# Output projections of retention heads 0 and 1 as one product of quarters in seven parts

## The chip, the cores and the metric

The kernel runs on one core of one Trainium2 chip. The time is that of the whole program on the device in microseconds (us), and three runs of the kernel before gave a median of 869.23 us (868.9 to 870.93). One more execution was taken with the hardware profiler: it took 870.49 us, and its span, from the first to the last instruction, is 868.7 us. The core has five engines that run side by side, each in the order of its own instructions: PE (TensorE, the matrix products), DVE (VectorE), ACT (ScalarE), POOL (GpSimd, here only a queue for transfers) and SP (SyncE, the queue for nearly all loads).

## The reference

The reference is a backbone of two layers over 512 tokens of width 1024, with 256 context tokens in front, all in float32. Layer 0 is a retention mixer with four heads, layer 1 a gated mixer in chunks of 128 tokens. The change touches the end of layer 0:

```python
ox, _, _ = retention_bidirectional(qx, kx, vx, log_g, s_f, s_b)   # (1, 4 heads, 512 tokens, 512)
out_x = retention_output(ox, zx, w_out)

def retention_output(o, z, w_out):
    o = o * lax.rsqrt(jnp.mean(o * o, axis=-1, keepdims=True) + NORM_EPS)
    b, h, l, dv = o.shape
    o = o.transpose(0, 2, 1, 3).reshape(b, l, h * dv).astype(z.dtype)
    return (o * jax.nn.silu(z)) @ w_out            # w_out: (4 heads * 512, 1024)

x = x + gate_x[:, None] * out_x
```

The product with `w_out` is a sum over the heads: each head adds its normalised and gated output (512 tokens by 512) times its own 512 rows of `w_out`.

## The kernel before

**Numbers as pairs.** A float32 number is held as two values of the type float32r, a high and a low part, and a product of two such numbers takes three matrix instructions (`mm3`): low by high, high by low, high by high. Whatever goes into PE is therefore split first: ACT copies the high part (a CAST in the profile) and DVE subtracts it from the source to get the low part (`split`). Weights come from memory as tiles `raw` of 128 by 1024 numbers (512 KB) and are split into tiles `hl`, of which there are four (`HL = 4`), used in turn.

**Products in seven parts.** The large projections (query, key, value and gate of layer 0, the value and u/z projections of layer 1) are computed as products of two by two quarters with seven products in place of eight. Tokens and inner dimension of the activations are halved into A11, A12, A21, A22, the weights into B11, B12, B21, B22. The sums of quarters of the activations are S1 to S4, those of the weights T1 to T4. `Product.run` takes one of seven names at a time and multiplies: B11 by A11, B21 by A12, T1 by S1, T2 by S2, B22 by S4, T3 by S3, T4 by A22. Partial results are taken out of PSUM by ACT (`snap`) and joined to the later ones by DVE (`plus`); `done` is called with each finished quarter. In a pair (`PAIRED`), two such products go through the names side by side, so that each operand has twice the time to be made.

**The stream of weights.** `Stream` (`Q`) holds the order in which the quarters of the weights are consumed. `load` sends a raw tile as soon as one of its slots is free; `get` hands out the next split tile and has the splits of the two after it written; the sums T1, T2 and T4 are made by DVE in place (`Q.sum`), and T3 by a transfer that adds in place, issued by POOL (`Q.add`, line 186).

**The heads.** After all projections (their results lie in DRAM) comes a loop over the four heads, lines 1306 to 1311. `attend(h)` has six steps of scores (12 products of 128 by 256 on PE, then on DVE the factor of the decay, `pf`, then a split, `ph` and `pl`), and two steps behind each comes its product with the values (12 products of 128 by 512). Six steps are two halves of the tokens (`hf`) times three pairs of key tiles. When a half is done, `finish` squares it on ACT to get the norm, `gated` multiplies by norm and gate on DVE (`gt`), and `flip` turns it on PE with transposes and splits it into the operand `og`. `project_out(h)` multiplies `og` with the head's four tiles of `w_out`, half by half: 2 halves x 4 tiles x 2 columns of 128 x 12 = 192 products of 128 by 256. Each group of 12 is added by DVE to the tile `acc`, which was loaded with x: `acc = p * gate0 + acc` (line 1302).

**What runs beside it.** Loading and splitting of the next head's queries and keys (`load_qk`), values (`load_v`), its decay table (`decay`) and its output weights (`load_wo`) are generators. `aside` takes one step of one of them and pins its ACT and DVE instructions behind what was written last on that engine (`pinned`). `bg` makes the modulation vectors of both layers on DVE from a stream of rows (`ada_piece`); its last piece (gate of layer 1) runs beside the heads, a step at a time (`step`).

**What sets the order.** PE's instructions stay in the order of the text. On the other engines a planner (the compiler's tile scheduler) picks, whenever it thinks an engine free, the instruction that is ready and stands first in the text; only pinned instructions and those behind a fence keep to the order of the text among themselves. All waits come from the tiles: a tile that takes a slot waits for the last reader of the tile before it in that slot. The slot is named by the tag in `st(shape, tag)`.

Nearly all compute instructions carry line 54 in the profile (the helper that records them), so groups are told apart by tile names.

Of the kernel before, what the change touches and what calls it, by code (L numbers as in the profile page):

```python
# [67 lines left out]
def hybrid_kernel(ctx, tc, xT_d, cT_d, cv_d, sv_d, rows_d, ada0_d, adag_d, w_d, rope_d, dec_d, ws_d, id_d, out_d):  # L68
# [21 lines left out]
    def lay(sizes, bufs=1):  # L90
        for tag, n in sizes.items():
# [4 lines left out]
         "sh1": 32, "shs": 16, "la": 32, "lb": 32, "lc": 32, "sum0": 16, "sum1": 16, "bns": 768, "mv": 32, "rv": 16})  # L96
# [6 lines left out]
    lay({"s0": 4096, "s2": 4096, "s3": 4096, "rope": 4096, "w6": 4096, "g2": 4096, "hl0": 8320})  # L103

    lay({"t2": 2048}, T2)
    lay({"hl1": 8320, "hl2": 8320, "hl3": 8320})
# [48 lines left out]
    class Stream:  # L155
# [23 lines left out]
        def add(self, must=None):  # L179

            for e in list(self.due):
                q = e[0]
                if (q, "22") in self.raws and (q == must or self.tick > e[1]):
                    self.due.remove(e)
                    self.added.add(q)
                    nc.gpsimd.dma_start(self.raws[q, "12"], self.raws[q, "22"], accum_op=ALU.add)  # L186
# [19 lines left out]
        def upto(self, n, late=None):  # L206

            while self.done < min(n, self.limit or len(self.items)):
# [4 lines left out]
                if name == "T3":  # L213
                    if q not in self.added:
                        self.add(q)
                    assert q in self.added
# [20 lines left out]
        def sum(self, n):  # L237
# [4 lines left out]
            if name == "T3" or name[0] not in ("T", "gated") or any((q, u) not in self.raws for u in uses):  # L242
                return
# [9 lines left out]
            if name == "T1":  # L253
                self.due.append((q, self.tick))
# [27 lines left out]
    def parts_of(q, u):  # L282
# [9 lines left out]
        if kind == "v1":  # L292
            return wide_parts(64 + 4 * i, kh, nh)
        return narrow_parts(80 + 2 * i + nh, 96 + 2 * i + nh, kh)
# [24 lines left out]

    FIRST_V1 = len(Q.items)  # L320
    V1_SLOTS = W + ["dec", "rope", "g0", "g2", "g3"]
    for a, b in ((0, 1), (2, 3)):
# [4 lines left out]
        for u in ("11", "21", "12", "22"):  # L327
            for cb in (a, b):
                Q.load((("v1", cb), u), V1_SLOTS, 2, parts_of(("v1", cb), u))

    def add_out(p, js=range(4)):
        for j in js:
# [3 lines left out]
            Q.load((q, "w"), W, 2, [(lambda r, e=e: r[:, 512 * e:512 * e + 512], w_d[112 + 4 * p + 2 * (j % 2) + e][:, h:h + 512])  # L336
# [3 lines left out]
    for i in range(UZ):  # L340
        Q.quad(("u", i), SINGLE)
        for u in RAWS:
            Q.load((("u", i), u), W, 2, parts_of(("u", i), u))
# [695 lines left out]
    def decay(h, tags=("w1", "g0")):  # L1039
        dt = dts[h] = st([P, TW], "dec", name="dt")  # L1040
        es = []
        for i in range(3):
# [8 lines left out]
            if n:  # L1051
                dve.tensor_tensor(dt[:, o:o + n], e[:, 0:n], e[:, 512:512 + n], ALU.mult)
# [703 lines left out]
```

## Time and profile before

| what | value |
| --- | --- |
| median of three runs | 869.23 us (868.9 to 870.93) |
| profiled execution, its span | 870.49 us, 868.7 us |
| PE busy | 858.7 us, 99% of the span |
| DVE busy | 698.8 us, 80% |
| ACT busy | 461.4 us, 53% |
| POOL busy | 78.1 us, 9% |
| scores and values of head 0 | 328.25 to 354.16 us |
| output projection of head 0 | 354.16 to 377.07 us |
| scores and values of head 1 | 377.07 to 403.34 us |
| output projection of head 1 | 403.34 to 426.26 us |
| heads 2 and 3 | 426.26 to 527.62 us |

The granted TensorE clock is 0.998 of full speed over the span. In the rows of groups "x12" counts instructions, the number behind the bar is their busy time in us and then the mean of one in ns; behind the second bar stands how long the engine was idle just before them and what ended most of that. In a timeline a row is a run of like instructions: start, length, engine, tiles written <- tiles read, count, and in brackets the idle time before it. Matrix instructions overlap, so the pace of PE is read from the distance of starts and not from the mean of one. "hl_e", "oA", "oS" and "og" are operands of PE, "pst" is any PSUM bank, "bg" a row tile of the modulation or decay stream.

### The profile page before, as it was taken

To read this page: it belongs to the slowest core of one execution; us is meant where nothing else is said; L and a number is where in the kernel's file an instruction comes from. 1 tells how busy PE (TensorE), PEld (TensorE's weight loads), DVE (VectorE), ACT (ScalarE), POOL (GpSimd) and SP (SyncE) were. 2 spreads that over 40 slices of the span, in tenths; PEclk is the share of its full clock that TensorE was granted. 3 is DMA by queue.
4 is the path that set the end of the run, shared out by engine and by line. 5 is a ranking of instruction groups with operands and counts; after the bars stand their busy time and mean duration, and the time that the engine had idled before them with its cause. 6 is when DMAs were issued, how large, how long until landed. Compare 5 with 4: busy or idle time off the path is not lost.

```text
span 868.7 us, 17062 instructions
## 1 busy us (share of the span) xinstructions
PE 858.7 (99%) x6870; PEld 822.4 (95%) x6870; DVE 698.8 (80%) x1007; ACT 461.4 (53%) x724; POOL 78.1 (9%) x119
## 2 busy tenths in 40 slices
PE   8999999999999999999999999999999999999997
PEld 7899999999999999999989899999999899899986
DVE  4799899869968885878676669998888478678895
ACT  4566644464364445627363649744667456255434
POOL 0001211211211011000000002021000000000110
PEclk9999999999999999999999999999999999999999
DMA  9945857868967898757174623666556246156522
GB/s 356 405 128 149 255 179 258 263 205 234 308 187 227 248 320 297 249 168 248 55 232 133 216 51 110 218 161 216 171 146 192 51 147 204 39 146 194 121 43 104
DMA packets 77551, 165.88 MB, mean 191 GB/s; under 512 B 8096, under 2 KB 33184, under 8 KB 77472
## 3 DMA queue, kind: packets, MB, share of 16 engines
q1 hardware_dynamic: 65856, 128.40, 44.8%
q0 software_dynamic: 11184, 36.18, 16.0%
q8 instruction: 54, 0.88, 0.4%
q10 hardware_dynamic: 432, 0.20, 0.1%
q14 instruction: 25, 0.20, 0.1%
HBM read 128.58 MB, written 24.12 MB: 176 GB/s over the span
## 4 chain that ended last, share of the span: by engine, by line
PE 94%; DMA 2%; DVE 1%; ACT 1%; issue 1%; ACTq 0%; DVEq 0%
PE pst L54 94%; DMA bg<-in_dec_dram 1%; DMA ident<-in_id_dram 1%; ACT junk L54 0%; DMA bg<-in_adag_dram 0%; DVE o L54 0%; ACT bg L54 0%; DVE acc L54 0%; DVE v L54 0%; DVE ada_a L54 0%; ACT L54 0%; DVE hl L54 0%; ACT hl L54 0%; ACT fss L54 0%; DVE dt L54 0%
## 5 line engine op out<-in xcount | busy, mean ns | idle before, releaser
L54 DVE TENSOR_TENSOR hl<-raw,hl 128x1024 fp32r<-128x1024 f32 (+2 forms) x197 | 235.8, 1200 | 69.3 <-ACT hl L54 69.0
L54 ACT CAST hl<-raw 128x1024 fp32r<-128x1024 f32 (+2 forms) x197 | 202.1, 1030 | 142.2 <-PE pst L54 60.9
L54 PE MATMUL pst<-hl,oS 128*128 128x256 f32 x1152 | 135.0, 277 | 0.0
L54 PEld LDWEIGHTS pst<-hl,oS 128*128 128x128 f32 x1152 | 132.9, 188 | 0.8 <-ACT ctx L54 0.4
L54 PE MATMUL pst<-oS,hl 128*128 128x256 f32 x1104 | 132.2, 277 | 0.0
L54 PEld LDWEIGHTS pst<-oS,hl 128*128 128x128 f32 x1104 | 128.1, 188 | 0.8 <-issue 0.8
L54 PE MATMUL pst<-oA,hl 128*128 128x256 f32 x936 | 116.9, 280 | 0.1
L54 PEld LDWEIGHTS pst<-oA,hl 128*128 128x128 f32 x936 | 110.7, 188 | 2.0 <-ACT oS L54 0.4
L54 PE MATMUL pst<-hl,oA 128*128 128x256 f32 x768 | 92.4, 277 | 0.0
L54 PE MATMUL pst<-og,hl 128*128 128x256 f32 x768 | 91.1, 278 | 0.0
L54 PEld LDWEIGHTS pst<-og,hl 128*128 128x128 f32 x768 | 89.2, 188 | 0.3
L54 PEld LDWEIGHTS pst<-hl,oA 128*128 128x128 f32 x768 | 89.4, 188 | 0.0
L54 DVE TENSOR_TENSOR raw<-raw 128x1024 f32<-128x1024 f32 x69 | 84.2, 1221 | 0.8
L54 ACT ACTIVATE snap<-pst 128x512 f32<-128x512 f32 x75 | 44.7, 596 | 69.3 <-PE pst L54 69.3
L54 PE MATMUL pst<-v,ph 128*128 128x512 f32 x192 | 59.8, 392 | 0.0
L54 PE MATMUL pst<-hl,ya 128*128 128x512 f32 (+1 forms) x246 | 59.1, 386 | 0.0
L186 POOL DMA_DIRECT2D raw<-raw x23 | 20.1, 874 | 388.5 <-ACT hl_e L54 173.4
L54 PEld LDWEIGHTS pst<-hl,ya 128*128 128x128 f32 x246 | 45.3, 188 | 9.5
L54 DVE TENSOR_TENSOR snap<-snap,pst 128x512 f32<-128x512 f32 x69 | 47.1, 682 | 5.7 <-PE pst L54 5.5
L54 ACT CAST ph<-pf 128x512 fp32r<-128x512 f32 x24 | 14.8, 618 | 56.3 <-DVE pf L54 56.3
L54 PEld LDWEIGHTS pst<-v,ph 128*128 128x128 f32 x192 | 36.1, 188 | 7.1
L54 DVE SCALAR_TENSOR_TENSOR acc<-pst,gate,acc 128x256 f32<-128x256 f32 x64 | 29.3, 480 | 11.5 <-PE pst L54 11.4
(207 smaller groups left out, 1106.4 us busy)
## 6 DMA issues: line engine op xcount, KB each, us to landing
raw<-in_w_dram SPq DMA_DIRECT2D x224, 256.0 KB, 4.0
bg<-in_adag_dram SPq DMA_DIRECT2D x32, 512.0 KB, 5.1
raw<-raw POOLq DMA_DIRECT2D x23, 512.0 KB, 4.8
ada_w<-in_ada_dram SPq DMA_DIRECT2D x16, 512.0 KB, 8.5
raw<-in_w_dram SPq DMA_DIRECT2D x16, 512.0 KB, 4.7
bg<-in_dec_dram SPq DMA_DIRECT2D x12, 512.0 KB, 4.5
v<-snap POOLq DMA_DIRECT2D x16, 256.0 KB, 4.2
z<-snap POOLq DMA_DIRECT2D x16, 256.0 KB, 4.5
```

The costliest lines, as they stand in the source:

```text
L54: made = op(*args, **kw)
L186: nc.gpsimd.dma_start(self.raws[q, "12"], self.raws[q, "22"], accum_op=ALU.add)
```

## The change

The output projections of heads 0 and 1 are taken out of the loop over heads and become one product of an activation matrix of 512 tokens by 1024 (head 0's 512 and head 1's 512) with the 1024 by 1024 rows of `w_out` that belong to these heads. It is done in quarters (token half by head, head by half of the columns) with seven products, as a pair of two column groups (`OUT0`), 14 items of 24 matrix products. The scores and values of both heads now come first, in one run of 12 steps (`attend_two`), the output product behind both (`out_two`). Heads 2 and 3 stay as they were (`attend_one`, `project_out`).

What it moves and adds:

- `flip` no longer writes `og` but hands the turned half to a function of its quarter, which splits it (A11, A12, A22), keeps plain copies and makes the sums S1 to S4 on DVE and ACT, pinned in order.
- The weights of both heads go through the stream `Q`: 8 raw tiles as before, but 14 splits in place of 8, with sums T1 and T2 on DVE and T3 and T4 by adding transfers from POOL. Three raw tiles are loaded at step 7 and five at step 11, when the slots of head 1's queries and keys come free.
- The finished quarters are written to `acc` by ACT, scaled by `gate0` (`put`), in place of DVE's multiply-add; x is added to `acc` behind that by four transfers from POOL that add in place, in place of four plain loads from SP before.
- A plan (a dictionary of steps) says which generator steps run where. Head 1's values take slots of the `hl` tiles and its decay table the slots `s0` and `s2`. Head 2's queries and keys are loaded and partly split during the 12 steps, its values and decay table during the output product.
- `bg`'s last piece moves from heads 0 to 2 to heads 2 and 3.
- The stream's free slots are emptied behind the output product, so that the first loads of layer 1's weights later take the slots `dec`, `rope`, `g0`, `g2` and `g3` first.

The diff, cut to what matters:

```diff
+    OUT0 = (("wo", 0), ("wo", 1))
+    WO_RAWS = ["w0", "w1", "w2"]
+    for name in PAIRED:
+        for q in OUT0:
+            Q.item(q, name)
+    for u in ("11", "21", "12", "22"):
+        for q in OUT0:
+            Q.load((q, u), WO_RAWS + list(ODD), 2, parts_of(q, u))
...
+    def outward(bank, a, w, fresh):
+        for kt in range(4):
+            if kt == 2 and inside:
+                inside.pop(0)()
+            r = (a[:, 0, kt, :], a[:, 1, kt, :])
+            for s in range(2):
+                o = kt * HS + s * P
+                mm3(bank[:, s * HS:s * HS + HS], (w[:, 0, o:o + P], w[:, 1, o:o + P]), r, fresh and kt == 0 and s == 0, kt == 3)
...
+        ROOM = {"A11": "oS3", "S3": "oS4", "A12": "oA12", "A22": "oA22", "S1": "oA11", "S2": "oS1", "S4": "oS2"}
...
+        def turn(h, hf, flipped):
+            act.pinned = dve.pinned = True
+            (quarter_11, quarter_21, quarter_12, quarter_22)[2 * h + hf](flipped)
+            act.pinned = dve.pinned = False
+        def quarter_11(flipped):
+            halved_parts("A11", flipped)
+            for r, src in zip(plain("11", "w3"), flipped):
+                act.copy(r, src)
+        def quarter_21(flipped):
+            for r, src in zip(parts("11"), flipped):
+                dve.tensor_tensor(r, r, src, ALU.subtract)
+            for r, src in zip(plain("21", "dec"), flipped):
+                act.copy(r, src)
+            halved("S3", at["11"])
+        def quarter_12(flipped):
+            halved_parts("A12", flipped)
+            for r, x, src in zip(plain("12", "g1"), parts("11"), flipped):
+                dve.tensor_tensor(r, x, src, ALU.subtract)
+        def quarter_22(flipped):
+            for r, src in zip(parts("21"), flipped):
+                dve.tensor_tensor(r, src, r, ALU.subtract)
+            halved("S1", at["21"])
+            for r, src in zip(parts("11"), flipped):
+                dve.scalar_tensor_tensor(r, src, -1.0, r, ALU.mult, ALU.subtract)
+            halved("S2", at["11"])
+            for r, src in zip(parts("12"), flipped):
+                dve.tensor_tensor(r, src, r, ALU.add)
+            halved("S4", at["12"])
+            halved_parts("A22", flipped)
...
+        plan = {(0, 2): [q, q, q, d], (1, 2): [d, v], (2, 2): [d, q, v], (3, 2): [q, q, v], (4, 1): [q], (5, 2): [v],
+                (6, 2): [q, v, q2, q2, q2], (7, 1): [v, raws], (8, 1): [v], (10, 1): [q2, q2],
+                (11, 2): [more, ahead(1)], (12, 2): [q2, ahead(2)]}
+        return attend((0, 1), plan, turn)
+    def out_two(flip, works):
+        def put(c):
+            def done(name, t):
+                th, nh = int(name[0]) - 1, int(name[1]) - 1
+                for s in range(2):
+                    m = 2 * (c + 2 * nh) + s
+                    act.activation(acc[:, m, th * HS:th * HS + HS], t[:, s * HS:s * HS + HS], AF.Copy, scale=gate0[:, m:m + 1])
+            return done
+        def turned():
+            flip()
+            between_modes()
+        prods = {q: Product(outward, put(q[1])) for q in OUT0}
+        n = 0
+        for name in PAIRED:
+            for q in OUT0:
+                w = Q.get()
+                if n == 1:
+                    inside.append(turned)
+                prods[q].run(name, w)
+                for work in works.get(n, ()):
+                    aside(work)
+                n += 1
+        Q.free[:] = []
+        for c in range(4):
+            nc.gpsimd.dma_start(acc[:, 2 * c:2 * c + 2, :], xT_d[:, 2 * c:2 * c + 2, :], accum_op=ALU.add)
...
-                if then is None and hf == 1 and c < 3:
+                if then is None and hf == 1:
                     step()
...
+    qs, ds, vs = load_qk(2), decay(2, ("w3", "g1")), load_v(2)
+    flip = attend_two(load_qk(1), load_v(1), decay(1, ("w3", "g1")), qs)
+    out_two(flip, {6: (vs, ds), 8: (vs, qs), 9: (ds,), 10: (vs, qs), 11: (vs, ds), 12: (vs, qs), 13: (vs, vs)})
     Q.limit = None
-    for h in range(HEADS - 1):
-        qs, vs = load_qk(h + 1), load_v(h + 1)
-        og, flip = attend(h, qs, vs)
-        project_out(wos.pop(h), og, flip, (decay(h + 1), vs, qs))
-    og, flip = attend(HEADS - 1, iter(()), iter(()))
+    qs, vs = load_qk(3), load_v(3)
+    og, flip = attend_one(2, qs, vs, load_wo(2), (2, 3, 5, 6))
+    project_out(wos.pop(2), og, flip, (decay(3, ("s0", "s2")), vs, qs))
+    og, flip = attend_one(3, iter(()), iter(()), load_wo(3), (0, 1, 2, 3, 5, 6))
```

In `attend` of both versions the flip of a half comes two steps behind its last value product; in the run of 12 steps that is at steps 6, 9 and 12 (`if i % 3 == 0 and pend`), and the fourth half is turned inside the second item of the output product (`turned`, called by `outward` after half of its matrix products).

More of the change, by code (lines that the diff above doesn't have):

```diff
@@ L1037, in hybrid_kernel, with decay @@
     dts = {}
[L1039 to L1040 removed]
+    def decay(h, tags):
+        if h == 1:
+            xt, ct = st([P, XW], "s0", name="dt"), st([P, CW], "s2", name="dt")
+        else:
+            whole = st([P, TW], "dec", name="dt")
+            xt, ct = whole[:, 0:XW], whole[:, XW:]
+        dts[h] = xt, ct
         es = []
@@ L1262, in attend @@
                 continue
-            if i == len(steps):
+            if i % 3 == 0 and pend:
                 flip()
-            aside(qs)
-            if i > 4:
-                aside(vs)
-            if (h, i) == (0, 2):
-                sp.pinned = True
-                for c in range(4):
-                    load(acc[:, 2 * c:2 * c + 2, :], xT_d[:, 2 * c:2 * c + 2, :])
-                sp.pinned = False
-            if i < 5:
-                aside(wo)
-            if i in (3, 5, 6):
-                step()
@@ L1277, in attend, with attend_one @@
-        return og, flip
+            run((i, 2))
+        return flip
+    def attend_one(h, qs, vs, wo, steps):
+        og = [st([P, 2, 4, HS], tag, F32R, name="og") for tag in ("oS3", "oS4")]
+        def turn(h, hf, flipped):
+            for fp, src in enumerate(flipped):
+                split((og[hf][:, 0, 2 * fp:2 * fp + 2, :], og[hf][:, 1, 2 * fp:2 * fp + 2, :]), src)
+        of = lambda work: lambda: aside(work)
+        plan = {(5, 0): [of(qs), of(wo)]}
+        for i in range(8):
+            plan[i, 2] = [of(qs)] + ([of(vs)] if i > 4 else []) + ([of(wo)] if i < 5 else []) + ([step] if i in steps else [])
+        return og, attend((h,), plan, turn)
```

172 lines of the change are left out of this document (112 added, 60 removed).

## The prediction

> **What bounds the kernel now.** I read the page first, then PE's waits, then the timeline of PE over heads 0 and 1, then each engine's busy time by stage.
>
> ```profile
> span 868.7 us, 17062 instructions
> PE 858.7 (99%) x6870; PEld 822.4 (95%) x6870; DVE 698.8 (80%) x1007; ACT 461.4 (53%) x724; POOL 78.1 (9%) x119
> PE 94%; DMA 2%; DVE 1%; ACT 1%; issue 1%; ACTq 0%; DVEq 0%
> ...
> PE pst L54 <- DMA ident<-in_id_dram: 1.9, 1, 1.9
> ...
> PE pst L54 <- DVE pf L54: 0.2, 1, 0.2
> ```
>
> PE is busy for 858.7 of 868.7 us, and the chain that ended last is PE for 94%. The one wait of PE among the heads is that of 0.2 us for `pf`. So a matrix product that is left out shortens the span by its pace on PE, unless its operands come late.
>
> ```profile
> 354.16 5.61 PE L54 MATMUL pst<-og,hl 128*128 128x256 f32 x48
> 359.61 1.03 PE L54 MATMUL pst<-ident,gt 128*128 128x128 f32 x8
> 360.40 0.95 PE L54 MATMUL pst<-og,hl 128*128 128x256 f32 x6
> 361.19 0.38 PE L54 MATMUL pst<-ones 128*128 128x128 f32 x2
> 361.33 15.90 PE L54 MATMUL pst<-og,hl 128*128 128x256 f32 x138
> 377.07 2.88 PE L54 MATMUL pst<-qk 128*128 128x256 f32 x24
> 380.17 1.65 PE L54 MATMUL pst<-qk 128*128 128x256 f32 x12 [0.22 <-DVE pf L54]
> ```
>
> This is head 0's output projection. From start to start 48 products take 5.45 us and 138 take 15.74 us, 113.5 and 114.1 ns each; I use 113.8. A flip costs 0.79, the two products on `ones` behind it 0.14.
>
> **The change, part by part: PE.** Two projections of 192 products become 14 items of 24, 336 in all: 48 x 0.1138 = 5.46 us less. The four flips of the two heads remain, three now among the scores; one pair on `ones` goes, 0.14. Head 1's scores follow head 0's in one run, so the start of head 1 with its 0.22 goes. Together 5.8 us. The output product lasts 336 x 0.1138 + 0.79 + 0.14 = 39.2 us. Counted from its start, item n begins at 2.73 n, and 0.93 later from item 2 on.
>
> **VectorE during the output product.** First what its operations take:
>
> ```profile
> L54 DVE TENSOR_TENSOR hl<-raw,hl 128x1024 fp32r<-128x1024 f32 x191 | 232.8, 1222 | 67.3 <-ACT hl L54 67.1
> L54 DVE TENSOR_TENSOR raw<-raw 128x1024 f32<-128x1024 f32 x69 | 84.2, 1221 | 0.8
> L54 DVE TENSOR_TENSOR snap<-snap,pst 128x512 f32<-128x512 f32 x69 | 47.1, 682 | 5.7 <-PE pst L54 5.5
> L54 DVE SCALAR_TENSOR_TENSOR acc<-pst,gate,acc 128x256 f32<-128x256 f32 x64 | 29.3, 480 | 11.5 <-PE pst L54 11.4
> L54 DVE TENSOR_TENSOR og<-pst,og 128x512 fp32r<-128x512 f32 x16 | 10.3, 685 | 0.5 <-ACT og L54 0.5
> ...
> 354.16:377.07 22.91, 2.37 (x5) 1.00 0.60 212
> ...
> 355.61 1.41 DVE L54 SCALAR_TENSOR_TENSOR gt<-pst,ss,z 128x512 f32<-128x512 f32 x2
> ```
>
> The row with 2.37 (x5) is the decay table of one head. Two of the 14 splits lie ahead of the product. What is left for VectorE inside it, in us: 12 low halves 14.7; four sums T1 and T2 4.9; six joins at 0.682 4.1; six quarter sums behind the last flip 4.1; low halves of S1, S2, S4 3.7 and of A22 1.4; `gt` 1.4; of head 2 the values 3.7, two key tiles 1.4 (like hl's and og's shapes) and the decay table 2.4. Taken out: 32 additions to `acc`, 15.4. The sum is 41.8 us in 45 instructions. Instructions in a queue overlap in the records: two `gt` of 0.745 take 1.41, 0.08 less each, so the sum is 41.8 - 3.6 = 38.2 of 39.2 us. VectorE is nearly full there. Has this kernel had that without loss?
>
> ```profile
> core 0: us, PE busy (x) PEld busy (x) DVE busy (x) ACT busy (x) POOL busy (x), PEclk, DMA share, GB/s
> 354.16:377.07 22.91, 22.91 (x204) 22.91 (x202) 17.64 (x31) 10.67 (x18) 0.00 (x0) 1.00 0.60 212
> 403.34:426.26 22.92, 22.92 (x204) 22.92 (x203) 18.52 (x33) 11.81 (x20) 0.00 (x0) 1.00 0.44 156
> 426.26:475.68 49.42, 49.42 (x360) 46.20 (x359) 34.65 (x57) 24.73 (x40) 0.00 (x0) 1.00 0.50 160
> 540.00:560.00 20.00, 20.00 (x173) 19.99 (x172) 20.00 (x27) 17.01 (x25) 1.93 (x4) 1.00 0.58 187
> 560.00:580.00 20.00, 20.00 (x177) 20.00 (x177) 20.00 (x30) 9.62 (x12) 4.30 (x7) 1.00 0.80 226
> ```
>
> From 540 to 580 us VectorE is full for 40 of 40 us, making S1 to S4 beside a pair of products just as here, and PE has no idle time. So a full VectorE alone costs nothing; late operands would. The tightest point is item 8 (B22 by S4), at 22.8: until then VectorE owes 1.4 for `gt`, seven low halves 8.6, four sums 4.9, two joins 1.4, six quarter sums 4.1, three S halves 3.7, in all 24.1 less 24 x 0.08 = 22.2 of 22.8. This holds only if the three waits for ScalarE's high halves of S1, S2 and S4 are filled with weights' work. Bounds: 0 if they are, 3.1 (three times 1.05, the cast below) if none is. I take 0.5, near the filled case, because the trace just shown is nearest to it.
>
> The fourth flip comes 36 products after the last value product (item 0 and half of item 1, 4.1 us) where it came after 48 (5.45). `gt` ended at 357.02, 2.86 after 354.16. Of the slack 1.2 us remain, so it costs nothing; VectorE brings little backlog there: steps 8 to 11 of the scores last 4 x 4.2 and hold four `pf` and `pl`, two pairs of `gt`, one quarter's sums and some splits, by the rows above about 14 us. Without that cover each us late is a us on PE.
>
> **ScalarE during the output product.**
>
> ```profile
> L54 ACT CAST hl<-raw 128x1024 fp32r<-128x1024 f32 x191 | 199.4, 1048 | 142.2 <-PE pst L54 60.9 <-DVE raw L54 54.0 <-issue 18.6
> L54 ACT ACTIVATE snap<-pst 128x512 f32<-128x512 f32 x75 | 44.7, 596 | 69.3 <-PE pst L54 69.3
> L54 ACT ACTIVATE f<-acc,gs 128x256 f32<-128x256 f32 x4 | 2.0, 507 | 0.3 <-DVE acc L54 0.3
> ```
>
> The stage of one projection took 10.7 to 11.8 us of ScalarE (rows above), with head-to-head work that stays. Added: 12 casts 12.6, six snaps 3.6, 16 scaled writes at 0.507 (the nearest form) 8.1, three S halves 3.1: 38.6, less 37 x 0.08, about 35.6 of 39.2. It fits.
>
> [...]
>
> **Start of head 2.** The values of head 2 are split at items 12 and 13, pinned behind these items' writes to `acc`. How a head started before:
>
> ```profile
> 331.29 0.69 DVE L54 TENSOR_TENSOR pl<-pf,ph 128x512 fp32r<-128x512 f32 x1 [0.74 <-ACT ph L54]
> ...
> 332.48 0.39 PE L54 MATMUL pst<-v,pl 128*128 128x512 f32 x1
> ```
>
> `pl` was done 0.5 us before the first value product read it. Now, after the end of item 13, ScalarE has two writes (0.9) and two casts of values (2.0) ahead of the first `ph`, and VectorE two low halves; `ph` ends at about 3.5, a low half in front delays `pl` to 4.9, and the product wants it at 4.1, three score groups in. I take 0.9. Bounds: 0, if the planner puts scores first, and 2.3, both low halves in front.
>
> **Moved to where it is hidden.** Eleven steps of the gate of layer 1 go to heads 2 and 3: VectorE is busy 34.65 of 49.42 us in head 2, room for seven additions of about 1.2. The transfers:
>
> ```profile
> raw<-raw POOLq DMA_DIRECT2D x23, 512.0 KB, 4.8
> acc<-in_xT_dram SPq DMA_DIRECT2D x4, 512.0 KB, 6.7
> ...
> L54 ACT CAST hl_e<-raw x4: 1043/1046/1048, 494.6 to 514.3; 128x1024 fp32r<-128x1024 f32 x4
> ```
>
> x is added by four transfers on POOL behind the last write; POOL has nothing else until layer 1. Head 2's projection reads `acc` about 27 us later (one attention as 377.07 to 403.34), and four in a row at 6.7 would take 27; side by side far less. I take 0; one after the other and slow, about 5 at most. T3 and T4 by transfer (4.8) have at least five items of time. SP loses four loads; the five late weight tiles queue behind head 1's scores, with over 12 us until T2 needs the last. Layer 1's first loads now wait for head 3's decay table and keys; the casts that started at 494.6 slip some us, with the first use past 527: 0, at most 1. A gain beyond PE's products is excluded, since PE waits for nothing else here.
>
> **Sum.** -5.8 + 0.5 + 0.9 = -4.4: span 864.3. The profiled execution would be 870.49 - 4.4 = 866.1; it lay 1.26 above the median of 869.23, so the median becomes 864.8.
>
> **Rivals.** *VectorE's gaps stay empty:* 3.1 in the product and 2.3 at head 2 give back 5.4 of 5.8: 868.8. For it: 38.2 of 39.2. Against: 540 to 580 us.
>
> *Slower, by order:* the sums behind the last flip are pinned in a row, and if the planner keeps the low halves of T1's weights behind them, T1 waits. From the flip's first bank (4.5): six sums 3.6, three casts 2.9, three halves 3.4, A22 1.7, hand-overs 0.7 end at 16.8, then cast and low half 2.2: 19.0 against item 4's start at 11.85. That is 7.2, with the same rule at head 2 2.3: 869.2 - 5.8 + 9.5 = 872.9. It makes the kernel slower once waits pass 8.4. Against it:
>
> ```profile
> 333.88 0.68 DVE L54 SCALAR_TENSOR_TENSOR pf<-pst,dt 128x512 f32<-128x512 f32 x1
> 334.48 1.22 DVE L54 TENSOR_TENSOR hl<-raw,hl 128x1024 fp32r<-128x1024 f32 x1
> ```
>
> A weight's low half, later in the text, is placed ahead of the scores' `pl`.
>
> *The x transfers are not hidden:* 5 us of wait at head 2's projection, 864.8 + 5 = 869.8.
>
> **Chances.** Forecast 0.66, empty gaps 0.20, slower by order 0.11, x late 0.03. Differences under 0.3% (2.6 us) can't be told from no change here. The forecast is faster; of the empty gaps a tenth, 0.02, would stay faster, 0.18 with x late's 0.03 is no change: faster 0.68, same 0.21, slower 0.11. Range: all gain and no cost is 863.4, less 0.4 for the spread of runs, 863.0; the upper end 870.5 takes in empty gaps and x late and leaves out slower by order.
>
> **What would show it.** Right: 336 products `pst<-hl,` on the quarters at 113 to 114 ns, the stage from the first score of head 0 to the first of head 2 some 93 us instead of 98.0 (328.25 to 426.26), PE waits under 2 us there, VectorE over 95% busy in the product. Wrong: PE idle at items 4 to 8 on `hl` or `oA`/`oS`, more than 1 us at head 2's first value product, or `acc` on a transfer.

## The result, and the profile after

The changed kernel takes 875.56 us in the median of five runs (873.71 to 877.23), against 869.23 (868.9 to 870.93) for the kernel before: a ratio of 1.0069, with a 95% interval of 1.0051 to 1.0088. The forecast was 864.8, so the change costs 6 us where it was to bring 4.4. The profiled execution took 875.56 us, its span is 873.8 us.

First the page of the changed kernel (span, busy times, chain) and the waits of PE among the heads:

```profile
span 873.8 us, 17037 instructions
PE 856.6 (98%) x6820; PEld 818.0 (94%) x6820; DVE 709.4 (81%) x1003; ACT 479.9 (55%) x757; POOL 84.8 (10%) x127
PE 81%; DVE 8%; DMA 7%; ACT 2%; issue 1%; DVEq 0%; SPq 0%; ACTq 0%
...
PE pst L54 <- DVE pf L54: 2.6, 1, 2.6
PE pst L54 <- DVE hl L54: 1.8, 1, 1.8
PE pst L54 <- DVE pl L54: 0.8, 1, 0.8
```

PE is busy 2.1 us less than before, not 5.8, and its share of the chain fell from 94% to 81%. Three new waits have appeared. PE's timeline shows where they stand:

```profile
388.27 11.47 PE L54 MATMUL pst<-oA,hl 128*128 128x256 f32 x96
399.58 2.99 PE L54 MATMUL pst<-oS,hl 128*128 128x256 f32 x24
404.42 15.93 PE L54 MATMUL pst<-oS,hl 128*128 128x256 f32 x120 [1.85 <-DVE hl L54]
420.18 5.82 PE L54 MATMUL pst<-oA,hl 128*128 128x256 f32 x48
425.84 4.40 PE L54 MATMUL pst<-qk 128*128 128x256 f32 x36
431.06 0.50 PE L54 MATMUL pst<-v,pl 128*128 128x512 f32 x1 [0.83 <-DVE pl L54]
...
476.03 2.88 PE L54 MATMUL pst<-qk 128*128 128x256 f32 x24
481.48 1.65 PE L54 MATMUL pst<-qk 128*128 128x256 f32 x12 [2.56 <-DVE pf L54]
```

The first wait is item 7 of the output product (T2 of the second column half), the second is head 2's first value product, the third is head 3's third group of scores. Besides the waits, the products themselves are slower than forecast, in two ways. 96 products take 11.31 us from 388.27 to 399.58, 117.8 ns each, where the forecast reckoned with 113.8. And behind the wait of 1.85 us the granted clock drops, as the stretches around it show (columns: stretch, busy time of each engine, granted clock, share of the DMA engines, GB/s):

```profile
core 0: us, PE busy (x) PEld busy (x) DVE busy (x) ACT busy (x) POOL busy (x), PEclk, DMA share, GB/s
328.28:425.84 97.56, 95.17 (x661) 88.46 (x659) 75.15 (x104) 65.02 (x109) 6.92 (x9) 0.98 0.62 186
402.00:405.00 3.00, 1.15 (x9) 0.95 (x9) 3.00 (x4) 1.95 (x3) 0.31 (x1) 0.96 1.04 324
405.00:407.00 2.00, 2.00 (x11) 2.00 (x11) 0.49 (x1) 1.24 (x1) 0.00 (x0) 0.50 1.06 240
```

PEclk is 0.50 from 405 to 407, and in all from 404.75 to 408.16, 3.41 us, which costs half of that, 1.7 us (an estimate). From head 0's start to head 2's start (328.28 to 425.84) it takes 97.56 us, against 98.01 before and about 93 in the forecast.

The account of the 5.1 us between the two spans: heads 0 and 1 gain 0.45; head 2 loses 0.8 (the 0.83 of wait and some 0.9 that the slow pace costs up to 449, less 0.92 of gate products that now stand in head 3); head 3 loses 3.8 (those 0.92, the wait of 2.56 and 0.3 more); layer 1's products lose 0.1; the tail behind the last product is 0.8 longer. That tail was between 5.9 and 6.8 us in all profiles, so the 0.8 is no more than its spread. Inside the first stage 5.8 were to be saved and 0.45 came. Given back are 1.85 at item 7, 1.7 of half clock, two waits of 0.27 at the flip, and a remainder of some 1.2, about what 300 products at 4 ns too much cost.

Why the operands are late is read from VectorE's timeline. First behind the last flip, then at head 3's start:

```profile
397.41 1.22 DVE L54 TENSOR_TENSOR oS<-quarter,oS 128x1024 fp32r<-128x1024 f32 x1
398.55 1.28 DVE L54 TENSOR_TENSOR oA<-pst,oA 128x512 fp32r<-128x512 f32 x2
399.74 1.21 DVE L54 TENSOR_TENSOR raw<-raw 128x1024 f32<-128x1024 f32 x1
400.88 4.62 DVE L54 TENSOR_TENSOR hl<-raw,hl 128x1024 fp32r<-128x1024 f32 x4
...
474.47 1.28 DVE L54 SCALAR_TENSOR_TENSOR ada_a<-bg,cpad,ada_a 128x1024 f32<-128x1024 f32 x1 [1.83 <-DMA bg<-in_adag_dram]
476.07 1.28 DVE L54 SCALAR_TENSOR_TENSOR ada_a<-bg,cpad,ada_a 128x1024 f32<-128x1024 f32 x1
479.54 1.28 DVE L54 SCALAR_TENSOR_TENSOR ada_a<-bg,cpad,ada_a 128x1024 f32<-128x1024 f32 x1 [1.41 <-DMA bg<-in_adag_dram]
480.74 0.68 DVE L54 SCALAR_TENSOR_TENSOR pf<-pst,dt 128x512 f32<-128x512 f32 x1
```

The low halves of S4 (`oS`) and A22 (`oA`), wanted by items 8 and 12, stand ahead of T2's second sum (`raw`), and the low half of item 7's weights is the third of the four `hl`. At head 3 two gate steps wait for their rows in the queue (1.83 and 1.41 us), and the factor of the scores, `pf`, stands behind them. In the kernel before, `pf` came 1.56 us behind head 3's start and no gate step stood there:

```profile
477.24 0.69 DVE L54 SCALAR_TENSOR_TENSOR pf<-pst,dt 128x512 f32<-128x512 f32 x1 [0.88 <-PE pst L54]
```

### The profile page after: what moved, and what is told of

It reads as the page before. It is cut to its first block, busy times and chain, and to the rows that moved or that the text cites. A ratio compares the mean times of both kernels' runs of the same rounds, so it can differ in the third digit from the quotient of the medians.

```text
span 873.8 us, 17037 instructions
## 1 busy us (share of the span) xinstructions
PE 856.6 (98%) x6820; PEld 818.0 (94%) x6820; DVE 709.4 (81%) x1003; ACT 479.9 (55%) x757; POOL 84.8 (10%) x127
## 4 chain that ended last, share of the span: by engine, by line
PE 81%; DVE 8%; DMA 7%; ACT 2%; issue 1%; DVEq 0%; SPq 0%; ACTq 0%
PE pst L54 81%; DMA ada_w<-in_ada_dram 2%; DVE hl L54 2%; DMA cq<-in_cT_dram 1%; DVE v L54 1%; DMA bg<-in_adag_dram 1%; DVE gt L54 1%; DMA qk<-q 1%; DMA bg<-in_dec_dram 1%; DVE ada_a L54 1%; DMA vt<-vt 1%; DVE quarter L54 1%; DMA raw<-in_w_dram 1%; DVE pf L54 0%; DMA cv<-in_cv_dram 0%
## 5 line engine op out<-in xcount | busy, mean ns | idle before, releaser
L54 DVE TENSOR_TENSOR hl<-raw,hl 128x1024 fp32r<-128x1024 f32 (+2 forms) x203 | 242.5, 1199 | 71.8 <-ACT hl L54 71.3
L54 ACT CAST hl<-raw 128x1024 fp32r<-128x1024 f32 (+2 forms) x203 | 208.3, 1031 | 155.7 <-PE pst L54 70.6
L54 PE MATMUL pst<-oS,hl 128*128 128x256 f32 x1296 | 157.4, 280 | 2.3 <-DVE hl L54 1.8
L54 PEld LDWEIGHTS pst<-oS,hl 128*128 128x128 f32 x1296 | 152.5, 190 | 3.6 <-DVE hl L54 2.1
L54 PE MATMUL pst<-oA,hl 128*128 128x256 f32 x1080 | 134.3, 280 | 0.1
L54 PEld LDWEIGHTS pst<-oA,hl 128*128 128x128 f32 x1080 | 127.8, 188 | 2.0 <-ACT oS L54 0.4
L54 PE MATMUL pst<-og,hl 128*128 128x256 f32 x384 | 46.6, 280 | 0.0
L54 PEld LDWEIGHTS pst<-og,hl 128*128 128x128 f32 x384 | 45.0, 188 | 0.4 <-DVE og L54 0.3
L54 PEld LDWEIGHTS pst<-qk 128*128 128x128 f32 x288 | 35.8, 188 | 3.9 <-DVE pf L54 2.8
L54 PE MATMUL pst<-qk 128*128 128x256 f32 x288 | 36.8, 280 | 2.6 <-DVE pf L54 2.6
```

Of the source, the lines that this page charges most:

```text
L54: made = op(*args, **kw)
```

## The experiments

Fourteen kernels ran, beside runs of the kernel before on the same chip; ratios are to these runs. Four ask about one cause each, the other ten rebuild the order step by step.

**1. The two last quarter operands later.** S4 and A22 are made behind items 5 and 8, not pinned there.

```diff
-            for r, src in zip(parts("12"), flipped):
-                dve.tensor_tensor(r, src, r, ALU.add)
-            halved("S4", at["12"])
-            halved_parts("A22", flipped)
+            rest.extend((s4(), a22()))   # the same instructions, as generators
...
+                if n in (5, 8):
+                    aside(rest.pop(0))
```

> The changed kernel with S4 and A22 made after items 5 and 8 of the output product instead of right behind the last flip. Theory (order): T2's second sum and item 7's low half stood on VectorE behind S4 and A22, so PE waited 1.85 us at item 7, and the granted clock went to half for 3.4 us behind that wait (1.7 us lost). Then both go: no PE wait over 0.5 us between items 4 and 9, granted clock 1.00 in the stage, the stage from head 0's first score to head 2's first about 94 us instead of 97.6, the time about 3.5 us under the changed kernel's, 872. Rival (load): VectorE is simply full, and the wait moves to item 8, 9 or 10 with about the same 1.5 to 2 us; the time stays at 875.

876.55 us, ratio 1.0082 (1.0065 to 1.0099). The wait at item 7 and its half clock are gone (the 144 products from 398.87 on take 118.9 ns each), but there are two other waits, at items 12 and 13. PE's timeline, then the ScalarE and VectorE rows in front of the first of them:

```profile
417.92 3.06 PE L54 MATMUL pst<-oA,hl 128*128 128x256 f32 x24 [1.93 <-DVE snap L54]
421.87 3.10 PE L54 MATMUL pst<-oA,hl 128*128 128x256 f32 x24 [0.89 <-DVE hl L54]
...
411.35 1.28 ACT L54 ACT_TABLE_LOAD   x1 [2.75 <-DMA bg<-in_dec_dram]
...
414.02 0.69 DVE L54 TENSOR_TENSOR dt<-bg 128x512 f32<-128x512 f32 x1 [2.96 <-ACT bg L54]
```

So the order at item 7 was the cause of that wait, but mending it alone brings nothing. ScalarE now stands for 2.75 us in front of an exponential whose decay tile (`bg`) has not landed, VectorE behind it, and behind these the join that frees item 12's bank. At head 3's start PE now waits 2.9 us for `pf`, and head 3 is 2.2 us longer than in the changed kernel; the mean granted clock of this execution is 0.996 (0.995 there).

**2. Four gate steps out of head 3.** They go into head 2's output projection.

```diff
-                if then is None and hf == 1:
+                if then is None and (c < 3 if hf else c > 0):
                     step()
...
-    ... load_wo(3), (0, 1, 2, 3, 5, 6))
+    ... load_wo(3), (2, 3, 5, 6))
```

> The changed kernel with the steps of layer 1's gate set at both halves of head 2's projection and none at the first two steps of head 3. Theory: at head 3's start VectorE stood still for rows that had not landed (1.83 and 1.41 us) ahead of the first pf, and PE waited 2.56 us. Then that wait is under 0.3 us and the time about 2.5 us under the changed kernel's, 873; the output product keeps its wait of 1.85. Rival: VectorE has too little room in heads 2 and 3 for the eleven steps wherever they stand; the wait moves into head 2's projection or head 3's scores and the time stays at 875.

871.72 us, ratio 1.0023 (1.0010 to 1.0037); the wait of 2.56 is 0.50:

```profile
479.18 1.65 PE L54 MATMUL pst<-qk 128*128 128x256 f32 x12 [0.50 <-DVE pf L54]
```

This one edit is worth 2.5 us between the two spans, which both have the slow stretch behind item 7's wait of 1.85 us (the 120 products take 15.77 and 15.76 us), and 3.8 in the medians. Of these first four it is the only one that brought a gain.

**3. The gap at item 7 filled.** 24 products on `ones` (48 instructions in the trace) keep PE busy ahead of item 7.

```diff
+                if n == 7:
+                    pr = pt((P, P))
+                    for _ in range(24):
+                        mm(pr, ones, ones, start=True, stop=True, skip_group_check=True)
                 prods[q].run(name, w)
```

> The changed kernel with 24 small matrix products on a constant ahead of item 7, where PE waited 1.85 us. Nothing else is changed, so item 7's operand comes as late as before. [...] Then PE is busy in that wait, the clock stays at 1.00 and the output product is 1.5 to 2 us shorter than in the changed kernel, though the operand is as late. Rival: the clock falls by itself or by temperature or other load; then a stretch of half clock is there in this run too, at another place or the same, and the time stays at 875.

875.71 us, ratio 1.0078 (1.0057 to 1.0100).

```profile
401.56 5.52 PE L54 MATMUL pst<-ones 128*128 128x128 f32 x48
406.84 13.86 PE L54 MATMUL pst<-oS,hl 128*128 128x256 f32 x120
```

No half clock shows behind the filling: the 120 products there take 13.7 us up to 420.54, 114.2 ns each. So the half clock at item 7 came with the idle time and not with the work. The filling takes 5.3 us itself. What it spares is some 3.9: the wait of 1.85, and 2.1 on the 120 products, which took 15.76 us in the changed kernel. So the stage is 1.0 us longer (98.55), and the time stays.

**4. A pair of products on `ones` inside item 2.**

```diff
                     inside.append(turned)
+                if n == 2:
+                    inside.append(between_modes)
```

> The changed kernel with one more pair of products on the constant tile of ones inside item 2. Theory (pace): behind the last flip, which was interrupted by two waits of 0.27 us, products of 128x256 follow each other at 117.8 ns instead of 113.4, until something interrupts the rhythm again; the pair sets it back. Then items 3 to 13 run at 113.4, 264 products by 4.4 ns, 1.2 us less, minus 0.14 for the pair. Rival: the pace belongs to the tiles that are read there, or to transfers beside it; then it stays at 117.8 and the time is 0.1 us longer.

877.55 us, ratio 1.0072 (1.0049 to 1.0095). The products behind the pair are quicker than in the changed kernel, 84 from 388.67 to 398.28 at 114.4 ns. This run doesn't show that the pair did it, because the twelve products ahead of it already ran at 114.2 ns (in the sixth kernel the pace changes at the pair, see the last section). And PE only runs earlier into the same late operand: the wait at item 7 is 2.27 instead of 1.85, and the 120 products behind it take 15.33 us (13.70 in the third kernel); the wait at head 3 is 3.4 instead of 2.56.

**5 and 6. Four edits of order together, without and with the pair.** Beside those of experiment 2: S4 and A22 behind items 5 and 7, now pinned; head 2's second and third value halves inside its attention; the later exponentials behind items 11 and 12.

```diff
-    out_two(flip, {6: (vs, ds), 8: (vs, qs), 9: (ds,), 10: (vs, qs), 11: (vs, ds), 12: (vs, qs), 13: (vs, vs)})
+    out_two(flip, {6: (vs, ds), 8: (vs, qs), 10: (vs, qs), 11: (ds, vs), 12: (ds, vs, qs)})
...
+            plan[0, 2].insert(0, of(own))       # own: head 2's value halves
+            plan[1, 2].insert(0, of(own))
...
+                if n in (5, 7):
+                    act.pinned = dve.pinned = True
+                    rest.pop(0)()
+                    act.pinned = dve.pinned = False
```

> The changed kernel with four edits of order and no edit of work: the fourth and seventh sum operands (S4, A22) made behind items 5 and 7 of the output product instead of behind the last flip, pinned there; head 2's second and third value halves made inside head 2's attention instead of ahead of it; the decay's exponentials of head 2 two items later; and four of the gate rows' steps moved out of head 3's start into head 2's output projection. Order theory (the loss is four waits for work that stands at the wrong place in VectorE's and ScalarE's queues): no wait of TensorE over 0.6 us between 386 and 500 us, no half clock there, head 2's start at about 422 us after the span's start instead of 425.8, head 2's own wait of 0.83 us gone, and the gate rows' 2 us as in the run with the rows alone: 867.5 to 869.5 us. Load theory (VectorE and ScalarE have too much to do in the product of quarters, so that a wait that is removed comes back further down): TensorE waits of 2 to 4 us in all between 402 and 432 us again and 871 to 873 us.

> The same, with one pair of small products of ones among the products of item 2, which in the run with the pair alone brought the products from 117.8 back to 113.4 ns. Pace theory: some 330 products between 388 and 449 us at 4.4 ns less each, 1.4 us less than the run without the pair, if no wait takes it: 866 to 868 us. Load theory: TensorE runs ahead only into longer waits for operands, and the time is that of the run without the pair.

873.86 us, ratio 1.0050 (1.0035 to 1.0065), and 873.54, 1.0043 (1.0027 to 1.0059). Head 2's own wait of 0.83 is gone (in the sixth kernel one of 1.00 for `pf` stands there), but the wait at item 12 has come back, as the load theory had it. SP's, ScalarE's, VectorE's and PE's rows of the fifth kernel give its chain:

```profile
407.22 0.38 SPq L54 DMA_DIRECT2D bg<-in_dec_dram  x1
...
412.41 1.28 ACT L54 ACT_TABLE_LOAD   x1 [4.29 <-DMA bg<-in_dec_dram]
...
415.07 0.69 DVE L54 TENSOR_TENSOR dt<-bg 128x512 f32<-128x512 f32 x1 [4.49 <-ACT bg L54]
416.99 0.68 DVE L54 TENSOR_TENSOR snap<-snap,pst 128x512 f32<-128x512 f32 x1
...
417.73 7.44 PE L54 MATMUL pst<-oA,hl 128*128 128x256 f32 x48 [2.22 <-DVE snap L54]
```

VectorE is idle for 4.49 us just before, so it isn't full there, and the load theory has the right place for a wrong reason. The tile goes into the buffer (`g1`) that holds the sum of the quarters 11 and 12 until S4 has been made of it. In the changed kernel this load was issued at 400.19; with S4 made later it is issued at 407.22.

**7 and 8. The two decay buffers changed over, with and without the pair.** The exponentials go back behind items 9 and 11.

```diff
-    qs, ds, vs = load_qk(2), decay(2, ("w3", "g1")), load_v(2)
+    qs, ds, vs = load_qk(2), decay(2, ("g1", "w3")), load_v(2)
```

> The last kernel (four edits of order and the pair) with one more: the two buffers of head 2's decay tiles change places, and the decay's exponentials stand behind items 9 and 11 again. In the kernel before this one the first decay tile went into the buffer that holds the sum of the quarters 11 and 12 until S4 is made of it, so that moving S4 back by 5 us moved this load from 400.2 to 407.2 us, its exponentials to 413.7, and the VectorE work behind them, a join of the product among it, to 417 us, where TensorE waited 1.5 to 2.2 us. Slot theory (the waits come from one chain by one buffer): the first decay tile lands before 402 us, the join of item 10 isn't late, no wait over 0.6 us between 402 and 432 us, head 2's start some 2.5 us earlier in its stage (stage of head 0's start to head 2's start 93 to 94.5 us) and 869 to 871 us. Load theory (VectorE and ScalarE are too full in the product): the 1.5 us comes back at another place of the same stretch and the time stays 872.5 to 874.5 us.

> The same without the pair of small products. Pace theory: products from 388 to 449 us at 117.8 instead of 113.4 ns, some 1.4 us more than with the pair. Otherwise: the same within 0.5 us.

870.08 us, ratio 1.0007 (0.9996 to 1.0019), and 870.58, 1.0007 (0.9997 to 1.0017). PE's timeline of the seventh kernel:

```profile
399.18 16.62 PE L54 MATMUL pst<-oS,hl 128*128 128x256 f32 x144
416.04 5.72 PE L54 MATMUL pst<-oA,hl 128*128 128x256 f32 x48 [0.24 <-DVE snap L54]
421.60 4.24 PE L54 MATMUL pst<-qk 128*128 128x256 f32 x36
```

Items 6 to 11 run through. From head 0's start at 328.09 to head 2's at 421.60 it takes 93.51 us, the length of the forecast, and without the pair 94.42. The slot theory holds, and 3.5 us are back. Yet the kernel only equals the one before, because head 2 now takes 51.18 us instead of 49.42 and head 3 53.50 instead of 51.94 (0.92 of it the gate products). ScalarE's row and the stretch ahead of head 2 show something new:

```profile
434.97 1.05 ACT L54 CAST hl<-raw 128x1024 fp32r<-128x1024 f32 x1 [1.26 <-DMA raw<-in_w_dram]
...
400.00:421.60 21.60, 21.36 (x187) 21.11 (x186) 16.45 (x23) 18.79 (x30) 2.53 (x3) 1.00 0.96 308
421.60:448.00 26.40, 25.85 (x154) 22.40 (x153) 20.46 (x28) 16.51 (x27) 0.83 (x1) 1.00 0.93 270
```

The DMA engines are busy for 0.96 and 0.93 of these stretches, where in the kernel before the projection ahead of head 2 had 0.44. A block of head 2's output weights comes late.

**9 and 10. x left out, and x in eight smaller transfers.** In the first x is missing from the result; both carry the pair.

```diff
-        for c in range(4):
-            nc.gpsimd.dma_start(acc[:, 2 * c:2 * c + 2, :], xT_d[:, 2 * c:2 * c + 2, :], accum_op=ALU.add)
...
+                # in the tenth kernel only, behind the two writes of a quarter
+                nc.gpsimd.dma_start(acc[:, x[0], x[1]], xT_d[:, x[0], x[1]], accum_op=ALU.add)
```

> The last kernel with the pair, without the four transfers that add x to the outputs of heads 0 and 1 (2 MB on POOL's queue); x is left out of the result. In that kernel the stage of heads 0 and 1 has the length that was forecast (93.5 us), and head 2's stage is 1.75 us longer than in the kernel before the change although it lost 0.92 us of gate products; in it ScalarE waits 1.26 us for a raw weight block of head 2's output projection (434.97), and the DMA engines, empty from 405 to 410 and at 0 to 20 per cent in the stretch before head 2 in the kernel before the change, are above 90 per cent from 407 to 440 us. Theory x (the x transfers hold up head 2's loads): ScalarE's wait for the weight block goes, head 2's stage comes down to 49.5 to 50.3 us and the time to 868 to 869.3 us. Rival (the gate rows and value halves that now stand in head 2 are what it costs): head 2's stage stays within 0.4 us of 51.2, and so does the time of 870.

> The same kernel with x added in eight transfers of 256 KB, each issued behind the two ScalarE writes of its quarter (from item 2 on, about 392 us) instead of four of 512 KB behind item 13. Theory x: the first four of them move into the stretch from 392 to 408 us, in which the DMA engines had room; a part of the gain of leaving x out, 0.3 to 1 us. Rival: nothing, or a loss, since the smaller transfers stand in POOL's queue ahead of the additions that make the weights of T3 and T4, and TensorE then waits at items 10 to 13.

868.11 us, ratio 0.9987 (0.9978 to 0.9996), and 874.77, 1.0058 (1.0046 to 1.0071). Without x ScalarE's wait for the weights is gone, and head 2 takes 50.07 us instead of 51.18, head 3 52.96 instead of 53.50. So in the mended order the transfers of x cost about 2 us in the medians, with intervals that just touch. Part of what head 2 still takes more than before is a wait of 0.91 us for `acc` in its projection, where the gate steps of experiment 2 now stand among the additions. (In the kernel before, the DMA engines were not empty from 405 to 410, as the expectation has it: their share there is 0.58, and 0.01 only from 420 to 425.) In smaller pieces and earlier they cost more: VectorE's idle time in front of the decay's second part becomes 3.99 us and PE waits 4.04 at item 12.

**11 and 12. x loaded ahead, VectorE writes.** In the eleventh kernel VectorE adds all sixteen pieces to x, as before the change; in the twelfth ScalarE still writes the first four and two transfers add their x.

```diff
-                    act.activation(acc[...], t[...], AF.Copy, scale=gate0[:, m:m + 1])
+                    dve.scalar_tensor_tensor(a, t[...], gate0[:, m:m + 1], a, ALU.mult, ALU.add)
...
+            sp.pinned = True                     # at step 7 of the scores of heads 0 and 1
+            for c in range(4):
+                load(acc[:, 2 * c:2 * c + 2, :], xT_d[:, 2 * c:2 * c + 2, :])
```

> One part of the change undone in the kernel with the five edits and the pair: VectorE writes the sixteen output pieces of heads 0 and 1 as a multiply-add on x, as in the kernel before, and x is loaded ahead of them during head 1's attention; no transfer adds x behind them. Leaving x out altogether took 2 us off that kernel. Queue theory (the x transfers behind item 13 are what delays head 2, and VectorE has room behind item 8: 16.5 of 21.6 us busy): 868 to 869.5 us. Rival (VectorE is full in the first part of the product: 18.6 of 19.5 us busy between 380.5 and 400 us, so four multiply-adds of 0.48 us there end as a wait of TensorE at items 6 to 8): a wait of 1 to 2 us at items 6 to 8 and 869.5 to 872 us.

> The same, but the four pieces that are ready first (quarter 11, behind items 2 and 3, where VectorE is full and the DMA engines are not) are written by ScalarE and take x from two transfers of 256 KB, and the other twelve, behind item 8, are VectorE's multiply-adds on x loaded ahead. Both theories agree here, if nothing else is in the way: no wait of TensorE over 0.6 us in the product, head 2's stage at 49.8 to 50.5 us, and 867.5 to 869 us, below the kernel before the change (869.2 to 869.9). If it stays at 870, the 2 us were not x's.

873.24 us, ratio 1.0047 (1.0034 to 1.0059), and 877.55, 1.0098 (1.0081 to 1.0115). Neither expectation held: items 6 to 8 don't wait, and item 12 waits 3.41 and 7.90 us. ScalarE's, VectorE's and PE's rows of the twelfth kernel:

```profile
418.50 1.33 ACT L54 ACTIVATE bg<-bg,lg 128x512 f32<-128x512 f32 x2 [8.20 <-DMA bg<-in_dec_dram]
...
420.80 1.23 DVE L54 TENSOR_TENSOR hl<-raw,hl 128x1024 fp32r<-128x1024 f32 x1 [7.22 <-ACT hl L54]
...
424.14 8.43 PE L54 MATMUL pst<-oA,hl 128*128 128x256 f32 x48 [7.90 <-DVE snap L54]
```

With ScalarE's writes behind item 8 gone the planner puts the second pair of exponentials ahead of the weights of later items in ScalarE's queue, and there they wait for their tile.

**13 and 14. The same two, with the exponentials behind item 13's weights.**

```diff
-    out_two(flip, {6: (vs, ds), 8: (vs, qs), 9: (ds,), 10: (vs, qs), 11: (vs, ds), 12: (vs, qs)})
+    out_two(flip, {6: (vs, ds), 8: (vs, qs), 10: (vs, qs), 11: (ds, vs), 12: (ds, vs, qs)})
```

> The kernel in which ScalarE writes the first four pieces and VectorE the other twelve on x loaded ahead, with one line changed: the second and third pair of the decay's exponentials stand behind the weights of item 13 in ScalarE's queue instead of ahead of those of items 12 and 13, where they waited for their tile's load (7.22 us in front of VectorE's low half of a weight, 7.9 us of TensorE). Theory (a late load in front of the weights; x's transfers the last part of the missing gain): no wait over 0.8 us at items 6 to 13, stage of heads 0 and 1 93 to 95 us, head 2 50 us, 867.5 to 869.3 us. Rival (the transfers are at their limit there, so what is not waited for at item 12 is waited for at head 2's start, where the decay tiles are used): a wait of 2 to 6 us at head 2's start and 871 to 875 us.

> The kernel in which VectorE writes all sixteen pieces on x loaded ahead, with the same line changed. Theory: as the other, with up to 0.5 us more for the four multiply-adds in VectorE's full stretch (the kernel it comes from had 0.48 instead of 0.29 us at the flip, and no wait at items 6 to 8): 867.5 to 869.8 us. Rival: 871 to 875 us, by a wait at head 2's start.

The mixed kernel takes 869.53 us, ratio 0.9998 (0.9987 to 1.0008); that with all pieces on VectorE 868.02, ratio 0.9973 (0.9960 to 0.9985). With x in the result it is the only one of the fourteen whose interval lies below the kernel before. Its page and PE's timeline:

```profile
span 866.6 us, 17029 instructions
PE 854.1 (99%) x6822; PEld 815.5 (94%) x6822; DVE 715.4 (83%) x1019; ACT 473.5 (55%) x741; POOL 81.5 (9%) x123
...
399.26 11.30 PE L54 MATMUL pst<-oS,hl 128*128 128x256 f32 x96
410.83 5.72 PE L54 MATMUL pst<-oS,hl 128*128 128x256 f32 x48 [0.27 <-DVE hl L54]
416.48 6.13 PE L54 MATMUL pst<-oA,hl 128*128 128x256 f32 x48
422.46 4.30 PE L54 MATMUL pst<-qk 128*128 128x256 f32 x36
```

One line takes 5 us off the eleventh kernel and 8 off the twelfth. The stage of heads 0 and 1 is 94.64 us, head 2 49.63. So the product of quarters can pay a little: 1.9 us in the medians, about a third of what its 48 products are worth. That is 0.27%, less than the 0.3% that the forecast took for no change, though the interval leaves out a ratio of 1. The pair on `ones` in item 2 has a share in it, 0.5 between the medians of the seventh and eighth kernel, whose intervals overlap. What separates the mixed kernel from the other is shown only in part: a wait of 0.49 us at head 2's start, and behind it the slow pace up to the flip in head 2's projection (the 48 products ahead of that flip take 118.5 ns each, 113.5 in the other kernel).

## Why the prediction was wrong

**"48 x 0.1138 = 5.46 us less": right.** Once the operands are in time, the stage is 93.51 us (seventh kernel, with the added pair), where the forecast said some 93.

**The 0.5 for VectorE in the product: wrong.** Its load was not too small: VectorE is busy for 35.6 us in the product, where 38.2 were reckoned. But the load stands in front. Up to 405.5 VectorE has no gap, and in the 20.3 us behind that it is busy for 10.9, so that it comes to 79% of the product and not to the 95% that the forecast named as its sign. The step that failed is the check of the tightest point. It looked at item 8 and at gaps, summed all that VectorE owes up to there, and took it that the right things are done first. At item 7 they weren't. The cost was 1.85 of wait and 1.7 of half clock, and the half clock was in no term of the sum. The rival "slower, by order" had this mechanism (pinned sums ahead of weights), but placed it at item 4 with 7.2 us.

**"1.2 us remain, so it costs nothing", for the flip: wrong, and small.** `gt` ended 5.0 us after the product's start (385.76 against 380.73), not 2.86, since a key tile and two low halves of weights stood ahead of it. PE waited 0.27 us for each of the two tiles.

**The pace of 113.8 ns: wrong.** It was taken from head 0's projection, which has two products on `ones` behind its flip; in the changed kernel the products behind the same pair ran at 117.8, and in the sixth kernel the 84 products behind a second pair at 114.6. Between the seventh and eighth kernel this is worth 0.9 us of the stage.

**"I take 0.9" for head 2's start: right.** The wait is 0.83, by the mechanism described, and it went when the value halves were moved.

**"Eleven steps of the gate ... room for seven additions": the second large miss.** Busy time says that VectorE has room, and it has. But each step waits in the queue for its rows, 1.83 and 1.41 us here, and the scores' `pf` stands behind it. The forecast named no queue behind these steps. Measured: 2.56 us of wait, and 2.5 between the spans when four of them were moved.

**"I take 0" for the transfers of x: not so.** In the changed kernel no wait of PE shows them, since other waits come first. In the mended order they cost about 2 us, and not by a wait for `acc`, which is where the forecast looked. That it goes by way of the DMA engines is argued: from 425 to 445 us they are busy for 0.96 with x (seventh kernel) and for 0.68 without, and ScalarE's wait of 1.26 us for a weight block is there with x and gone without. How POOL's transfers would slow SP's loads, though no instruction waits for them, no run here shows.

**Layer 1's loads, "0, at most 1": right.** Its products last 335.22 us against 335.14.

## What to carry over

A sum of busy times doesn't tell whether an edit is free. For each added instruction write down what it waits for itself (a row, a buffer, a tile of the engine in front) and what stands behind it in the same queue; both large errors here were of that kind, on VectorE, which was idle for microseconds nearby. When an operand is made later, look at who takes its buffer next: the load that inherits it becomes late too.

## What the runs showed of the chip that was not expected

**Half the clock behind a wait of 1.85 us, and not behind one of 2.56.** In the changed kernel PE's wait of 1.85 us ends at 404.42, and the granted clock is 0.50 from 404.75 to 408.16. Its wait of 2.56 us ends at 481.48, and there the clock stays at 1.00. In other kernels the slow stretch shows in how long the products behind a wait take. The 120 behind item 7 took 15.77 us in the second kernel (wait of 1.85 us) and 15.33 in the fourth (2.27), against 13.70 in the third, which has no wait there. The 48 behind the wait at item 12 took 7.27 us in the fifth (2.22) and in the eleventh (3.41), 8.47 in the tenth (4.04) and 8.27 in the twelfth (7.90), against 5.96 in the thirteenth, which has none. Behind the 1.93 us in the first kernel 24 products took 3.06 us, 0.23 more than at 117.8 ns each, where the half clock of the changed kernel cost 1.7. The length of the wait alone, then, does not tell whether it comes; what does is open. Of the second kernel's ten runs five have a mean granted clock of 0.999 and take 869.93 to 871.03 us, the other five have 0.996 or 0.997 and take 872.41 to 874.14. One stretch of 3.41 us at half clock lowers the mean by 0.002 (an estimate: half of 3.41 of 871 us), so by the mean it seems to come in some runs of the same kernel and not in others.

**Two paces of the same product.** At a granted clock of 1.00, products of 128 by 256 follow each other at 113.3 ns (36 of them from 475.68 to 479.76 in the kernel before) or at 117.8 (96 from 388.27 to 399.58 in the changed kernel). In the sixth kernel the pace changed at a pair of small products in their midst:

```profile
389.45 1.58 PE L54 MATMUL pst<-oA,hl 128*128 128x256 f32 x12
390.87 0.39 PE L54 MATMUL pst<-ones 128*128 128x128 f32 x2
391.01 9.79 PE L54 MATMUL pst<-oA,hl 128*128 128x256 f32 x84
```

The twelve ahead of the pair run at 118.3 ns, the 84 behind it at 114.6; in the thirteenth and fourteenth kernels it is 117.5 and 114.6. In the fourth and seventh the twelve ahead already ran at 114.2 and 113.3, behind the same flip and pair that were followed by 117.8 in the changed kernel. So a pair can bring the quick pace and does not always; what sets the pace is open.
